# Sums of weight blocks made in DRAM by transfers, five up tiles in seven products

## The chip, the cores and the metric

The kernel runs on one core of a Trainium2 chip. The metric is device time in microseconds, from the launch of the program to its end. A core has TensorE (PE in the profile, its weight loads PEld), VectorE (DVE), ScalarE (ACT), GpSimd (POOL) and SyncE (SP), each with its own queue of instructions, and 16 DMA engines that serve the queues of transfers. Each engine takes its queue in order: an instruction that waits holds up all behind it. In the profile a queue that issues transfers carries a q (SPq, POOLq).

## The reference

One layer of a hybrid block over 512 tokens of width 1024, all in float32: a combined input projection feeds three groups of attention heads (A: differential, B: with forget gates, C: chunked with a relative bias), one output projection, then a gated MLP with a causal depthwise convolution of width 3, then a gated embedding per layer. Cut to what matters here:

```python
def conv_gated_mlp(h, w_up, conv_w, conv_b, w_down):   # w_up 1024 x 5632, w_down 2816 x 1024
    u = h @ w_up
    up = jnp.pad(u, ((0, 0), (CONV_WIDTH - 1, 0), (0, 0)))
    c = conv_b
    for j in range(CONV_WIDTH):
        c = c + conv_w[j] * up[:, j:j + S]
    gate, val = jnp.split(c, 2, axis=-1)
    return (jax.nn.silu(gate) * val) @ w_down

h = x
z = rms_norm(h, ln_mix) @ w_in              # split into the heads of A, B and C
...
h = h + jnp.concatenate([o_a, o_b, o_c], axis=-1) @ w_out
h = h + conv_gated_mlp(rms_norm(h, ln_ffn), w_up, conv_w, conv_b, w_down)
gate = jax.nn.sigmoid(rms_norm(h, ln_ple) @ w_ple_gate)
h = h + (p @ w_ple_proj) * gate
```

## The kernel before

**Numbers.** A float32 product is made of three products in a shorter format. Each operand is split into a rounded part (hi) and a remainder (lo), and `mm3` (line 184) adds hi·hi, hi·lo and lo·hi. For weights ScalarE writes hi (a CAST in the profile) and VectorE the remainder, raw minus hi (a TENSOR_TENSOR w_lo); `split` (line 168) does it for the MLP, `load_w` (line 112) for the attention, where the remainder is at places made by GpSimd or by a transfer that adds.

**Attention.** The input projection is done in ten parts (A0, A0b, A1, A1b, B0 to B2, C0 to C2), each for four tiles of 128 tokens. One part for one token tile is a slot; a slot takes some 6 us. `run` (line 694) puts steps of the attention between the matmuls of a slot; the tables T and EARLY say which step begins in which slot. While one part is multiplied, the weights of the next are loaded by SyncE (`in_w`, four tiles of two blocks each) into a ring of four raw tiles and split. The order of ScalarE, VectorE, GpSimd and SyncE is made by a scheduler here; TensorE's order is that of the program. Normalisation of queries and keys (`qk_sums`, line 367), moves of them (`move`, line 390) and the scaling of probabilities run on GpSimd. Then come the output projection, the norm ahead of the MLP, and the projection of the embedding.

**Up projection.** 22 tiles f, each 128 columns of gate and 128 of value. A plain tile (`up_plain`, line 1237) is two groups of 8 blocks of weights times 3 products over 512 tokens: 48 matmuls of 512 columns. A tile of SEVEN (5, 10 and 15; `up_seven`, line 1261) does the same in the manner of Strassen, seven products of half the rows, half the columns and half the tokens instead of eight: 7 x 4 x 3 = 84 matmuls of 256 columns. It needs sums of weight blocks. `seven_weights` (line 1102) loads five tiles (3584 columns); three transfers on GpSimd's queue add blocks to them while they land (`add_of`), and four additions of GpSimd (`sum_of`) make the rest.

**Down projection.** The 22 tiles are four phases (PHASES 0, 6, 12, 18, 22). For each phase and each half n of the output there are seven products, over as many pairs of tiles as the phase has (18 matmuls of 256 columns, 12 in the last phase), each one added into h by VectorE (`add_h`, line 950). `down_weights` (line 1120) loads four blocks of weights and makes the four differences t1 to t4 on GpSimd (`diff`); each is then split. A difference of the last phase stands in tiles dn_a, dn_b, dn_t. Four products of phase 2 stand behind the last up tile, ahead of the products of phase 3, which need that tile. `cols3` (line 1518) transposes the finished h for the last stage.

**Order in the MLP.** Every piece is a Task. TensorE's order is the order in which tasks are made: `fill`, `downs`, `due` and AHEAD (lines 1470 to 1500) interleave plain pieces with pieces of sevens, and put phases 0 and 1 of the down projection in where their tiles are done. A planner at the end (line 1620 on) lays out the other engines: each task has a due time by TensorE's order, and on each engine the task is taken that can begin soonest, by written costs, and is due first. Raw weights go through a ring of six tiles, split ones through a ring of seven.

Of the kernel before, what the change touches and what calls it, by code (L numbers as in the profile page):

```python
# [8 lines left out]
F32 = mybir.dt.float32  # L9
# [38 lines left out]
AHEAD = 2  # L48

SEVEN = (5, 10, 15)  # L50
# [3 lines left out]
def kernel(ctx: ExitStack, tc: tile.TileContext, x, xt0, xt, pt_in, small, g_ffn_in, bias_c,  # L54
                             w_in, w_out, w_up, w_down, w_ple_gate, w_ple_proj, out):
# [56 lines left out]
    def load_w(src_fn, nk, m, n, name, eng=dve, gain=None, later=False):  # L112
# [3 lines left out]
        for dst, src in src_fn(raw):  # L116
            dma = nc.sync.dma_start(out=dst, in_=src)
            if later:
                tc.keep_in_program_order(dma)
# [247 lines left out]
    def qk_sums(z, t, name):  # L367
# [7 lines left out]
        (dve if name == "A0" else nc.gpsimd).tensor_scalar(rs[:, 0:4], rs[:, 0:4], rstd[:, t, 3:4], EPS, ALU.mult, ALU.add)  # L375
        nc.gpsimd.tensor_tensor(out=rs[:, 4:8], in0=rs[:, 0:4], in1=nhalf[:, 0:4], op=ALU.pow)
# [13 lines left out]
    def move(dst, src):  # L390
        nc.gpsimd.tensor_scalar(dst, f32(src), 1.0, 1.0, ALU.mult, ALU.mult)
# [121 lines left out]
    def head_bias(kind, hd):  # L513

        tb = ap.tile([P, S], F32, tag="bias", bufs=3, name=f"bias_{kind}{hd}")
        if kind == "A":
            nc.gpsimd.tensor_scalar(tb, dist, -SLOPES[hd], 1.0, ALU.mult, ALU.mult)
# [39 lines left out]
    def scores(pr, hh, qbs):  # L557
# [7 lines left out]
        for qb in qbs:  # L565
# [3 lines left out]
            if kind == "A":  # L569
                yield  # L570
                e2, st2 = softmax_map(QK[pr, 1], hh, qb, bq, rowb, f"{pr}_{hh}_{qb}b")
                nc.gpsimd.tensor_scalar(e2, e2, st2[:, 2:3], X["nlam"], ALU.mult, ALU.mult)
                dve.scalar_tensor_tensor(e, e, st[:, 2:3], e2, ALU.mult, ALU.add)
            else:
                nc.gpsimd.tensor_scalar(e, e, st[:, 2:3], 1.0, ALU.mult, ALU.mult)
# [205 lines left out]

    slot = 0
# [14 lines left out]
    for j, (pr, part, *_) in enumerate(PARTS[1:], 1):  # L797
# [18 lines left out]
    for n in range(2):  # L816
        for t in range(NT):
# [9 lines left out]
            slot += 1  # L827
    split_o(7, 8, slice(0, S))
# [101 lines left out]
    L1A, L2A, L2B, L3, L1, L2, L4 = range(7)  # L930
    G, LEFT = {}, {}

    def left_tiles(name):
# [3 lines left out]
    PRODUCTS = ((L1A, 0, "X", True), (L1, 4, "Y", True), (L2, 5, "X", False), (L4, 2, "Y", False),  # L937
                (L3, 6, "X", False), (L2A, 1, "Z", True), (L2B, 3, "X", False))
# [8 lines left out]

    ADDS = {0: ((0, 0),), 1: ((1, 1),), 2: ((0, 1),), 3: ((0, 1),), 4: ((1, 1),), 5: ((0, 0),), 6: ((1, 0),)}

    def add_h(n, j, acc):  # L950
        for b, c in ADDS[j]:
            dve.tensor_tensor(out=hblk(b, n, c), in0=hblk(b, n, c), in1=pv(acc), op=ALU.add)
# [102 lines left out]
    def again(r, name, deps):  # L1055

        w = Weights()
        w.n, w.raw, w.load, w.name = r.n, r.raw, r.load, name
        v = r

        def do():
            w.hi, w.lo = split(v.t, w.n)

        w.hi_slot = Slot("hi")
        w.split = Task("do", [AC(w.n), DV(w.n)], do, (w.load, *deps), [w.hi_slot], [w.raw])
        return w

    def add_of(w, c0, c1, src, deps=(), uses=()):

        def do():  # L1070
            pool.dma_start(out=w.t[:, c0:c1], in_=src(), accum_op=ALU.add)

        return Task("add", [("pool", 0.9), ("acc", (c1 - c0) * 0.0025)], do, (w.load, *deps), (), (w.raw, *uses))

    def sum_of(w, c0, w2, c1, n, deps):

        def do():
            d = w.t[:, c0 : c0 + n]
            pool.tensor_tensor(out=d, in0=d, in1=w2.t[:, c1 : c1 + n], op=ALU.add)

        return Task("do", [("pool", 0.3 + n * 0.0021)], do, (w.load, w2.load, *deps), (), {w.raw: 0, w2.raw: 0})

# [19 lines left out]
    def seven_weights(f):  # L1102

        size = (768, 768, 768, 768, 512)
        ws = [tile_of(n, f"ws{f}_{i}", w_up[f][:, 768 * i : 768 * i + n]) for i, n in enumerate(size)]
        src = w_up[f]
# [4 lines left out]
        for w, deps in zip(ws, ((), (), a, a, b)):  # L1111
            split_of(w, deps)
        order = (0, 1, 4, 3, 5, 6, 2)
# [4 lines left out]
    RIGHT = {"a1": 0, "t1": 4, "t2": 5, "b2": 2, "t3": 6, "a2": 1, "t4": 3}  # L1118

    def down_weights(ph, n, name, tag="raw"):  # L1120

        m = w_down[ph].shape[4]
        src = {what: w_down[ph][n, i, j] for what, (i, j) in (("a1", (0, 0)), ("b1", (0, 1)), ("b2", (1, 1)), ("a2", (1, 0)))}
        raw = {what: tile_of(m, f"{name}_{what}", src.get(what), tag) for what in ("a1", "b1", "b2", "t2", "a2")}

        place = {what: what for what in raw}
        wrote, read = {what: [q.load] for what, q in raw.items()}, {what: [] for what in raw}

        def diff(what, to, a, b):

            a, b, place[what] = place[a], place[b], to

            def do():
                x, y, z = (raw[q].t[:, :m] for q in (to, a, b))
                pool.tensor_tensor(out=x, in0=y, in1=z, op=ALU.subtract)

            q = Task("do", [("pool", 0.3 + m * 0.0021)], do, wrote[a] + wrote[b] + wrote[to] + read[to], (),
                     list({raw[p].raw: 0 for p in (to, a, b)}))
            for p in (a, b):
                read[p].append(q)  # L1140
# [222 lines left out]
    def down(ph, n, tags):  # L1363
        d = Down((ph,), n, tags)
        for what in RIGHT:
            d.product(what)
# [372 lines left out]
```

## Time and profile before

| | us |
|---|---|
| runs, lowest to highest | 727.92 to 728.24 |
| runs, median of 3 | 728.09 |
| profiled execution | 727.97 |
| its span, first to last instruction | 726.2 |
| TensorE busy | 706.1 |
| VectorE busy | 553.0 |
| ScalarE busy | 393.8 |
| GpSimd busy | 270.9 |
| granted TensorE clock | 0.999 |

The span holds the attention up to about 300 us, the MLP from there to about 660, and the gate of the embedding to the end. Line numbers in the profile are those of the kernel; since the engines are called through a helper, most instructions have its line, L78, and are told apart by the names of their tiles: u is the sum of an up tile, s and su those of a tile in seven products, dn_X, dn_Y, dn_Z those of the down projection, w_raw, w_hi and w_lo weights of the MLP, A_r to C_r raw weights of the attention. In a group's row stand, after the bar, the busy time and the mean of one in ns, then the idle time ahead of the group and what ended it.

### The profile page before, as it was taken

The page shows a single profiled execution, that of the slowest core. Times are in us where ns is not written, and L with a number is a line of the kernel's source. Part 1 is how long each engine was busy: PE and PEld are TensorE (multiplying, and loading weights), DVE is VectorE, ACT ScalarE, POOL GpSimd, SP SyncE. Part 2 cuts the span into 40 slices and gives each one's busy share as a digit, 9 for nine tenths or more (in the row PEclk, how much of TensorE's full clock was granted, in tenths as well). Part 3 has the DMA queues.
Part 4 walks back from the last instruction along what each step waited for, and adds up shares of the span by engine and source line. Part 5 has one row for each costly group of instructions (what it writes and reads, how often), then busy time and mean ns, then how long its engine had stood idle before and what let it go on. Part 6 is the DMA issues. An engine that isn't in the chain of part 4 may idle for free. (4 is left out here: it accounts for less than half of the span.)

```text
span 726.2 us, 11876 instructions
## 1 busy us (share of the span) xinstructions
PE 706.1 (97%) x4219; PEld 633.7 (87%) x4219; DVE 553.0 (76%) x1085; ACT 393.8 (54%) x745; POOL 270.9 (37%) x359
## 2 busy tenths in 40 slices
PE   9998999999999999999999999999999999999997
PEld 8987989998999887889888899888998888899886
DVE  7678787887877855758978768787898779988552
ACT  6646775865766664564655544543444543544821
POOL 5676676756665640212101144031520004361400
PEclk9999999999999999999999999999999999999999
DMA  9443425404211135564445434562254322123441
GB/s 332 172 136 110 120 63 124 138 30 110 88 48 56 59 63 165 171 210 90 138 138 125 102 100 123 139 159 66 88 175 117 95 87 82 57 73 94 156 129 58
DMA packets 36806, 83.22 MB, mean 115 GB/s; under 512 B 4198, under 2 KB 5990, under 8 KB 36748
## 3 DMA queue, kind: packets, MB, share of 16 engines
q1 hardware_dynamic: 32700, 73.52, 32.3%
q0 software_dynamic: 3760, 8.66, 6.4%
q8 instruction: 33, 0.54, 0.3%
q10 hardware_dynamic: 288, 0.30, 0.1%
q14 instruction: 25, 0.20, 0.1%
HBM read 74.19 MB, written 4.21 MB: 108 GB/s over the span
## 5 line engine op out<-in xcount | busy, mean ns | idle before, releaser
L78 DVE TENSOR_TENSOR w_lo<-w_raw,w_hi 128x768 fp32r<-128x768 f32 (+1 forms) x118 | 114.9, 993 | 21.9 <-ACT w_hi L78 21.2
L78 ACT CAST w_hi<-w_raw 128x768 fp32r<-128x768 f32 (+1 forms) x118 | 89.6, 786 | 71.1 <-POOL w_raw L78 33.0
L78 PE MATMUL u<-Tl,w_hi 128*128 128x512 f32 (+1 forms) x336 | 125.6, 374 | 0.8 <-DVE Tl L78 0.8
L78 PE MATMUL u<-Th,w_hi 128*128 128x512 f32 (+1 forms) x336 | 125.7, 374 | 0.6 <-ACT pps L78 0.6
L78 PE MATMUL u<-Th,w_lo 128*128 128x512 f32 (+1 forms) x336 | 125.4, 373 | 0.0
L78 POOL TENSOR_TENSOR w_raw<-w_raw,w_raw 128x768 f32<-128x768 f32 (+1 forms) x30 | 55.0, 1854 | 143.7 <-DVE w_lo L78 112.8
L78 PEld LDWEIGHTS u<-Tl,w_hi 128*128 128x128 f32 x336 | 63.1, 188 | 13.0 <-DVE Tl L78 1.2
L78 PEld LDWEIGHTS u<-Th,w_hi 128*128 128x128 f32 x336 | 63.1, 188 | 12.9 <-ACT pps L78 1.0
L78 PEld LDWEIGHTS u<-Th,w_lo 128*128 128x128 f32 x336 | 63.1, 188 | 12.5
L78 DVE SCALAR_TENSOR_TENSOR c<-u,cols,c 128x511 f32<-128x511 f32 x76 | 56.7, 747 | 18.6 <-ACT c L78 17.4
L78 POOL DMA_DIRECT2D w_raw<-in_w_up_dram x9 | 7.9, 912 | 100.2 <-DMA w_raw<-in_w_up_dram 100.2
L78 ACT ACTIVATE c<-u,cols 128x512 f32<-128x512 f32 x38 | 29.5, 776 | 21.7 <-PE u L78 21.7
L78 PE MATMUL dn_X<-w_hi,g_ah 128*128 128x256 f32 x144 | 40.7, 283 | 0.3 <-DVE h L78 0.3
L78 PE MATMUL dn_X<-w_lo,g_ah 128*128 128x256 f32 x144 | 40.7, 283 | 0.3 <-DVE w_lo L78 0.3
L78 PE MATMUL dn_X<-w_hi,g_al 128*128 128x256 f32 x144 | 40.6, 282 | 0.0
L78 PE MATMUL B_z<-B_h,Th 128*128 128x384 f32 x96 | 34.6, 360 | 0.6 <-DVE B_zn L78 0.6
L78 PE MATMUL C_z<-C_h,Th 128*128 128x384 f32 x96 | 34.3, 358 | 0.0
L78 PE MATMUL C_z<-C_l,Th 128*128 128x384 f32 x96 | 32.3, 337 | 0.0
L78 PE MATMUL B_z<-B_h,Tl 128*128 128x384 f32 x96 | 32.3, 337 | 0.0
L78 PE MATMUL C_z<-C_h,Tl 128*128 128x384 f32 x96 | 32.3, 337 | 0.0
L78 PE MATMUL B_z<-B_l,Th 128*128 128x384 f32 x96 | 32.3, 337 | 0.0
L78 PEld LDWEIGHTS dn_X<-w_hi,g_ah 128*128 128x128 f32 x144 | 27.1, 188 | 0.8 <-ACT w_hi L78 0.5
(484 smaller groups left out, 2145.6 us busy)
## 6 DMA issues: line engine op xcount, KB each, us to landing
w_raw<-in_w_up_dram SPq DMA_DIRECT2D x50, 384.0 KB, 3.7
w_raw<-in_w_down_dram SPq DMA_DIRECT2D x24, 384.0 KB, 3.1
w_raw<-in_w_up_dram SPq DMA_DIRECT2D x22, 256.0 KB, 3.4
B_r<-in_w_in_dram SPq DMA_DIRECT2D x12, 384.0 KB, 3.4
C_r<-in_w_in_dram SPq DMA_DIRECT2D x12, 384.0 KB, 3.2
wo_r<-in_w_out_dram SPq DMA_DIRECT2D x16, 256.0 KB, 2.9
w_raw<-in_w_ple_gate_dram SPq DMA_DIRECT2D x16, 256.0 KB, 2.9
h<-in_x_dram SPq DMA_DIRECT2D x4, 512.0 KB, 7.0
```

What stands on the lines that cost most here:

```text
L78: ins = getattr(self.eng, op)(*a, **k)
```

## The change

The sums and differences of weight blocks are added up in DRAM while the attention runs. Nine jobs do it: one for each of five up tiles, one for each of four down phases. A job copies four blocks from DRAM to a DRAM tile on SyncE's queue, then adds four blocks to it by three transfers on GpSimd's queue, one step every three slots. JOBS says in which slots: three jobs begin at slots 10, 11 and 12, three at 18 to 20 and three at 26 to 28. The copies of an up tile move 1.05 MB, those of the phases 3.15 MB each and 2.10 MB for the last one; together 16.8 MB are copied and 16.8 MB added, by nine issues of SyncE and 27 of GpSimd.

In the MLP the weights of a seven are then two loads of weights and three of sums, without transfers that add and without additions; a down product loads its block of weights or of sums (seven loads for each half and phase) and splits it, without subtracts on GpSimd. The form of the seven products of the down projection is another, with as many additions into h, some of them subtracts.

SEVEN is 4, 7, 10, 12 and 15 instead of 5, 10 and 15. TensorE's order in the MLP is written out in a string: P is a piece of a plain tile, S of a seven, D a product of the down projection. Behind the last up tile stand five products of phase 2 instead of four. The transposes cols3 of the first half stand one product further back.

The order of TensorE in the attention stays as it was. In the order that SyncE gets, the copies have no wait of their own: those of the up tiles 4 and 7 and of phase 0 stand between the loads of A1b, those of 10, 12 and 15 between loads of B1, those of phases 1 to 3 among the loads of C0.

```diff
-AHEAD = 2
-SEVEN = (5, 10, 15)
+ORDER = ("PPPPSSPSSSPSPPPPSSPSSSPSPPPDDDDDDDDDDDDDDPSSPSSSPSPSSPSSSPSPPPPSSPSSSPSPDDDDDDDDDDDDDDPPPPPPPPPPPPPPPPP")
+SUMS_FROM, SUMS_STEP = 10, 8
+PLAIN, SEVEN = tiles_of(ORDER)
+JOBS = {}
+_jobs = [("u", f) for f in SEVEN] + [("d", ph) for ph in range(len(PHASES) - 1)]
+_jobs.sort(key=lambda q: q[1] if q[0] == "u" else PHASES[q[1] + 1] + 3)
+for _i, _q in enumerate(_jobs):
+    for _k in range(4):
+        JOBS.setdefault(SUMS_FROM + _i // 3 * SUMS_STEP + _i % 3 + 3 * _k, []).append(_q)
...
+    def sum_job(key):
+        if key[0] == "d":
+            ph = key[1]
+            m = w_down[ph].shape[4]
+            src, more = w_dsum[ph], w_dadd[ph]
+            v = DSUM[ph] = dp.tile([P, 4, 2, m], F32, tag=f"dsum{ph}", name=f"dsum{ph}")
+        else:
+            f = key[1]
+            src, more = w_usum[f], w_up[f][:, 1024:2048].rearrange("p (i c) -> p i c", i=2)
+            USUM[f] = v = dp.tile([P, 4, 512], F32, tag=f"usum{f}", name=f"usum{f}")
+        with tc.issue_after(sp.last):
+            nc.sync.dma_start(out=v, in_=src)
+        for a, what in ((slice(1, 3), lambda: more), (0, lambda: v[:, 1]), (3, lambda: v[:, 0])):
+            yield
+            with tc.issue_after(pool.last):
+                nc.gpsimd.dma_start(out=v[:, a], in_=what(), accum_op=ALU.add, max_dma_last_dim=6144)
+        yield
+
+    def next_job():
+        for key in JOBS.get(slot, ()):
+            if key not in SUMS:
+                SUMS[key] = sum_job(key)
+            next(SUMS[key])
...
             run(in_unit(pr, part, n, t, ws, pre[t]), steps.get(slot, []))
             slot += 1
+            next_job()
...
-    PRODUCTS = ((L1A, 0, "X", True), (L1, 4, "Y", True), (L2, 5, "X", False), (L4, 2, "Y", False),
-                (L3, 6, "X", False), (L2A, 1, "Z", True), (L2B, 3, "X", False))
+    PRODUCTS = {"1e": (0, "X", True, 1, 0, ALU.add), "S1": (3, "Y", True, 0, 1, ALU.subtract), "S2": (4, "X", False, 0, 0, ALU.add),
+                "1o": (2, "Z", True, 1, 0, ALU.add), "1e2e": (5, "X", False, 0, 1, ALU.subtract), "1oS2": (1, "Y", False, 0, 0, ALU.add),
+                "2o": (6, "X", False, 1, 1, ALU.subtract)}
...
     def seven_weights(f):
-        ws = [tile_of(n, f"ws{f}_{i}", w_up[f][:, 768 * i : 768 * i + n]) for i, n in enumerate(size)]
-        a = [add_of(ws[2], 512, 768, lambda: src[:, 1024:1280]), add_of(ws[3], 0, 768, lambda: src[:, 1280:2048])]
-        sums = [(2, 0, 2, 512), (2, 256, 3, 0), (3, 256, 2, 512), (3, 512, 3, 0)]
-        a += [sum_of(ws[i], c0, ws[j], c1, H, a) for i, c0, j, c1 in sums]
-        b = [add_of(ws[4], 0, 512, lambda: src[:, 2048:2560])]
+        usum = USUM[f].rearrange("p i c -> p (i c)")
+        ws = [tile_of(n, f"ws{f}_{i}", w_up[f][:, 768 * i : 768 * i + n] if i < 2 else usum[:, 768 * (i - 2) : 768 * (i - 2) + n]) for i, n in enumerate(size)]
...
     def down_weights(ph, n, name, tag="raw"):
-        def diff(what, to, a, b):
-                pool.tensor_tensor(out=x, in0=y, in1=z, op=ALU.subtract)
...
+        src = {f"{c + 1}{'eo'[i]}": w_down[ph][n, i, c] for i in range(2) for c in range(2)}
+        src.update({what: DSUM[ph][:, i, n] for i, what in enumerate(("S2", "S1", "1e2e", "1oS2"))})
+        return lambda what: split_of(tile_of(m, f"{name}_{what}", src[what], tag))
...
+    FIRST = ("1e", "S1", "1o"), ("1e", "S1")
+    for c in ORDER:
+        next(pieces[c])
...
+    d1.product("1e", (3,))
     cols3(0, 0)
     cols3(1, 0)
-    d1.product("a1", (3,))
+    d1.product("S1", (3,) if "S1" in FIRST[1] else None)
```

More of the change, by code (lines that the diff above doesn't have):

```diff
@@ L827 @@
             slot += 1
+            next_job()
+    assert all(next(q, None) is None for q in SUMS.values())
     split_o(7, 8, slice(0, S))
@@ L945, in pv, with add_h @@
         return t.rearrange("p (b c) -> p b c", b=2)
[L948 to L952, printed above, removed]
+    def add_h(n, what, acc):
+        _, _, _, b, c, op = PRODUCTS[what]
+        dve.tensor_tensor(out=hblk(b, n, c), in0=hblk(b, n, c), in1=pv(acc), op=op)
     ple_cols()
```

184 lines of the change are left out of this document (67 added, 117 removed).

## The prediction

> **What bounds the kernel now.** I read the page's first lines, then busy time by stretches, then the chain of waits, then the groups of each engine, and last the queues and the sequence of SyncE and ScalarE.
>
> ```profile
> span 726.2 us, 11876 instructions
> PE 706.1 (97%) x4219; PEld 633.7 (87%) x4219; DVE 553.0 (76%) x1085; ACT 393.8 (54%) x745; POOL 270.9 (37%) x359
> ```
>
> TensorE is busy for 706.1 of 726.2 us. A change can pay by giving it less work or by closing its 20 us of gaps. Where those lie is in the stretches:
>
> ```profile
> core 0: us, PE busy (x) PEld busy (x) DVE busy (x) ACT busy (x) POOL busy (x), PEclk, DMA share, GB/s
> 40.00:140.00 100.00, 93.36 (x580) 86.46 (x579) 80.28 (x244) 66.21 (x157) 68.19 (x97) 1.00 0.43 112
> 140.00:240.00 100.00, 98.64 (x610) 93.54 (x609) 81.24 (x259) 67.13 (x168) 63.23 (x103) 1.00 0.23 67
> 340.00:520.00 180.00, 180.00 (x1041) 157.34 (x1040) 145.08 (x205) 89.18 (x134) 41.82 (x31) 1.00 0.44 120
> 520.00:540.00 20.00, 19.67 (x166) 19.50 (x165) 18.58 (x22) 8.32 (x12) 8.04 (x4) 1.00 0.47 139
> 540.00:620.00 80.00, 80.00 (x369) 65.48 (x368) 66.22 (x90) 36.43 (x54) 10.17 (x5) 1.00 0.36 107
> 620.00:640.00 20.00, 18.52 (x151) 17.90 (x150) 18.24 (x25) 9.74 (x15) 5.25 (x4) 1.00 0.17 54
> 640.00:660.00 20.00, 19.18 (x164) 18.98 (x163) 17.82 (x19) 9.57 (x15) 14.80 (x8) 1.00 0.12 40
> ```
>
> The clock is 1.00 in each stretch, so a matmul saved is worth its full time. The attention (40 to 240) has 8.0 us of gaps. The up tiles have none: 180.00 of 180.00 and 80.00 of 80.00. The down projection has 0.33 + 1.48 + 0.82 = 2.6 us. What ends those gaps is in the chain of waits (columns: start, length, engine, tile, how many):
>
> ```profile
> 537.44 2.13 PE dn_Y L78 x18
> 539.57 2.14 PE dn_X L78 x18
> 545.99 50.41 PE u L78 x216
> ...
> 628.32 1.12 POOL dn_a L78
> 629.46 0.63 ACT w_hi L78
> 630.12 1.54 DVE w_lo L78
> 631.83 0.35 issue
> 633.68 3.71 PE dn_X L78 x29
> ...
> 651.88 0.69 DVE h L78
> 652.61 0.65 PE n_t L78 x4
> ```
>
> At 628 TensorE waits on a subtract of two weight blocks by GpSimd (dn_a, 1.12 us), then on that block's rounding (w_hi) and remainder (w_lo). At 651.88 it waits for the last addition into h before the transposes n_t. Elsewhere the chain is TensorE itself.
>
> **The change part by part.**
>
> *Two more up tiles in seven products.* 216 matmuls of 512 columns took 50.41 us: 0.2334 each. 18 of 256 columns took 2.14: 0.1189 each. A plain tile has 48 of the first: 11.20 us. A tile in seven products has 84 of the second: 9.98. That is 1.22 less, for two tiles **−2.4 us**, all of it on the path, since TensorE has no gap there. The rest of its work, down projection included, keeps its count.
>
> *What the sevens ask of VectorE.*
>
> ```profile
> L78 DVE TENSOR_TENSOR w_lo<-w_raw,w_hi 128x768 fp32r<-128x768 f32 x85 | 90.8, 1084 | 14.9 <-ACT w_hi L78 14.4
> L78 DVE TENSOR_TENSOR su<-sX,su 128x256 f32<-128x256 f32 x12 | 4.8, 418 | 8.3 <-ACT su L78 8.3
> L78 DVE TENSOR_TENSOR w_lo<-w_raw,w_hi 128x768 fp32r<-128x768 f32 x10 | 9.6, 955 | 3.8 <-ACT w_hi L78 3.7
> L78 POOL TENSOR_TENSOR w_raw<-w_raw,w_raw 128x768 f32<-128x768 f32 x24 | 48.3, 2022 | 139.3 <-DVE w_lo L78 112.8 <-issue 21.7 <-DMA w_raw<-in_w_down_dram 4.4
> L78 POOL DMA_DIRECT2D w_raw<-in_w_up_dram x9 | 7.9, 912 | 100.2 <-DMA w_raw<-in_w_up_dram 100.2
> ```
>
> (The first two rows are of 340 to 660 us, the third of 545 to 598, the POOL rows of the whole run.) Each seven splits 3584 columns of weights instead of 2048: two more remainders of 768, 2 × 0.955 = 1.9, and four additions su of 0.418, 1.7. Together 3.6, for two tiles 7.2 us. VectorE had 180 − 145.08 = 35 us free in 340 to 520. It also gets time back: GpSimd's 24 subtracts (48.3 us) go, and with GpSimd almost still the remainder takes 955 ns, against 1084 in the mean beside them. 85 × 0.13 = 11 us. Net about nothing; I take 0. Without that relief the 7.2 us still fit into the 35 us; they would show only within one seven, at most 9.98 us long, where VectorE has about 12 us to do, and there a plain tile's slack has to follow it.
>
> The Trainium skill, page "GPSIMD Engine Reference", section 1 (Specifications), says that GpSimd shares its SBUF interfaces with VectorE and that instructions of VectorE with two inputs in SBUF contend for them. The 955 and 1084 ns agree; by that rule the relief goes to every such instruction, and the sum stays as it is since TensorE is what ends there.
>
> *Sums ready in DRAM: no subtract ahead of a product.* In the MLP 24 subtracts of GpSimd, three accumulates of each old seven and four additions beside them go, and the same number of columns or more is loaded instead. Down products then need a load and a split, as up tiles do, which show no gap. So the 628 stall loses its first link (1.12 us). Five products of phase 2 rather than four now stand ahead of the first one that needs the last up tile, which covers 2.14 us more. The 651.88 wait gets one product of cover by the move of the transposes behind the next product. Bounds: none of the 2.6 us, or all of it. VectorE is at 18.24 of 20 us in 620 to 640 and becomes what is late next. I take three quarters, **−2.0 us**. More loads in the down projection (seven per half and phase instead of four) lie where the DMA share is 0.44 or below; I take 0.
>
> *GpSimd in the attention.* 27 accumulates are issued from its queue, 0.912 us each by the row above: 25 us more on an engine busy for 68.19 + 63.23 of 200 us. Behind them wait the normalisations and moves of queries and keys that the attention runs on GpSimd. Each accumulate also waits for the step before it to land; with 3 slots between (about 18 us) that wait should be over. Bounds: nothing, or a fifth of it on the path, 5. If the 8.0 us of gaps grow with GpSimd's load, 8.0 × 25 / 131 = **+1.5 us**, which I take.
>
> *Nine copies from DRAM to DRAM on SyncE's queue, 16.8 MB, ahead of weight loads.* No run of before shows such a copy. The nearest rows are the loads at the start, and the accumulates of the output weights (stretches of 10 and 12 us):
>
> ```profile
> q1 hardware_dynamic: 1799, 4.00, 104.5%
> ...
> q0 software_dynamic: 576, 1.05, 54.6%
> ```
>
> The first gives 4.00 MB in 10.45 us of all engines: 383 GB/s. The second 1.05 MB in 6.55: 160 GB/s. So the copies take 44 to 105 us of all engines and the accumulates, as many bytes, 105. The engines are free for 57 + 77 us of 40 to 240 by the shares above, so two of these together do not fit if both are slow, and some work then waits. What can wait are the loads queued behind:
>
> ```profile
> 32.95 3.74 SPq L117 DMA_DIRECT2D A1b_r<-in_w_in_dram  x4
> 39.45 21.80 SPq L117 DMA_DIRECT2D B_r<-in_w_in_dram  x5
> 105.73 10.91 SPq L117 DMA_DIRECT2D C_r<-in_w_in_dram  x4
> ...
> 38.86 0.62 ACT L78 CAST A1b_h<-A1b_r 128x512 fp32r<-128x512 f32 x1 [2.30 <-DMA A1b_r<-in_w_in_dram]
> 39.66 1.15 ACT L78 CAST A1b_h<-A1b_r 128x512 fp32r<-128x512 f32 x2 [0.18 <-issue]
> 57.32 0.83 ACT L78 CAST B_h<-B_r 128x768 fp32r<-128x768 f32 x1
> 139.09 0.39 ACT L78 ACTIVATE B_e<-B_e,B_st 128x128 f32<-128x128 f32 x1
> ```
>
> SyncE issues in order and waits for nothing that a copy needs, so the copies start long before their slots: the first two of the up tiles and the first down phase (1.05, 1.05 and 3.15 MB) stand between the loads of A1b from about 34.6 on, the down phases 1 and 2 (3.15 each) between the loads of C at about 109 and 122. In the same queue the first load of B stands behind 5.8 MB. ScalarE rounds it at 57.32, and softmax work is queued behind ScalarE's wait.
>
> - At 383 GB/s: a load of A1b comes 1.05 MB or 2.7 us later; the second casts are asked for 0.8 us after the first, and the changed order puts them a few short instructions (some 0.9 us) further back: 1.0 late. B's first load lands by 51, on time. Phase 2 is copied by 122 + 8.2 = 130, ahead of ScalarE's need near 139. ScalarE waits 1 us.
> - At 230: A1b 4.6 − 1.7 = 2.9 late, B 34.6 + 25 + 1 = 60.7, 3.4 late, C 0 to 12, middle 6. About 12.3.
> - At 160: 4.9, 14 and some 20. About 39.
>
> Between no part and all of such a wait reaching TensorE (its projections run on weights loaded before), I take half. The copy is nearest to the load: the same queue, the same engines, whole rows. So 1 us, half of it: **+0.5 us**; ends 0 and +19.5.
>
> *Copies, by the skill.* The Trainium skill, page "DMA: Bandwidth & Descriptors", section "Latency and other measured facts", has copies between HBM tensors at 207 to 214 GB/s per direction when nothing slows them. No run of before shows it. By that figure the copies take an estimated 80 us, ScalarE waits about 17 us, and the time would be 727.97 − 2.9 + 8.5 = 733.6 us: the first rival below, which stands on the rows at 160 and 383 without it.
>
> *Sum.* −2.4 − 2.0 + 1.5 + 0.5 = −2.4 us on the profiled execution's 727.97 us (its span 726.2 and 1.8 around it): 725.6. The median of the runs, 728.09, is 0.12 above it, so the same sum stands for both; I say **725.6 us**.
>
> **The rivals.** Runs differ by under 0.2%, some 1.5 us: same is 726.6 to 729.5.
>
> *Late loads (slower).* Copies run nearer 160 than 383 GB/s because they read and write DRAM, and accumulates take their share at the same time. It decides from about 250 GB/s down: B's first load is on time as long as 5.8 MB take under 22 us (266 GB/s). At 230 the sum is 727.97 − 2.9 + 6.1 = 731.2, at 160 744.6. For it: the accumulates, which also move by reading twice, at 160. Against it: ScalarE's present wait of 2.30 us for A1b leaves TensorE's work in 40 to 140 at 93.36, so a wait is not passed on one to one. Chance 0.36.
>
> *Everything in the attention is hidden, the MLP gets all.* −2.4 − 2.6 and the seven tiles' relief let the gaps between sevens stay closed: 721 to 723.3. For it: 8.0 us of gaps with queues half idle. Against it: GpSimd at 68%. Chance 0.12.
>
> *The sevens do not gain.* Three of five sevens stand close together (tiles 10, 12, 15 as 4 and 7 do), VectorE at 12 us against 9.98 in each: five times up to 2 us lost takes the 2.4 and the 2.0. 727 to 729, same. Against it: 35 us free in 180. Chance 0.13; a worse form, where sums land late for the first seven and TensorE stands still, ends at 730 or more, chance 0.05.
>
> **How the numbers follow.** The forecast holds 0.34. Faster: 0.34 + 0.12 = 0.46. Same 0.13. Slower 0.36 + 0.05 = 0.41. Both signs hold much, so the range takes in the upper case but for its far end: 720.5 to 739. The likeliest case alone is 723.5 to 726.6.
>
> **What would show it.** TensorE's matmuls should be 72 more (2 × 84 − 2 × 48) and its busy time after 240 us about 2.4 lower. GpSimd should be nearly without tensor operations after 340, w_lo's mean nearer 955 ns. ScalarE's casts B_h near 57 and C_h near 139 should show no idle time put down to a load; if they show 3 us or more, the late loads have it. The stretch 40 to 240 should hold within 2 us of the old 8.0 us of gaps. I am wrong if copies hold queue q1 above 50 us of all engines, or if the first seven waits for its sums.

## The result and the profile after

The changed kernel takes 758.29 us (median of 4 runs, 755.55 to 760.38) against 728.16 before (median of 4): 1.0404 times as long, 95% interval 1.0387 to 1.0422. The forecast was 725.6 us with a range of 720.5 to 739. The profiled execution took 758.6 us with a span of 756.8.

The page of the kernel after, its first line and its busy times:

```profile
span 756.8 us, 12081 instructions
PE 715.2 (95%) x4291; PEld 641.9 (85%) x4291; DVE 536.2 (71%) x1097; ACT 399.2 (53%) x757; POOL 214.3 (28%) x335
```

TensorE has 72 matmuls more, as forecast, and yet is busy for 9 us longer. Busy time by stretches of the kernel after shows why (columns as in the prediction; the second last is the share of the 16 DMA engines):

```profile
core 0: us, PE busy (x) PEld busy (x) DVE busy (x) ACT busy (x) POOL busy (x), PEclk, DMA share, GB/s
40.00:140.00 100.00, 89.96 (x548) 83.07 (x547) 76.28 (x207) 60.36 (x142) 72.00 (x101) 0.98 0.95 257
140.00:160.00 20.00, 11.55 (x60) 8.77 (x59) 7.79 (x46) 5.07 (x16) 7.44 (x11) 0.93 1.04 281
160.00:180.00 20.00, 14.66 (x75) 12.62 (x74) 11.28 (x39) 11.44 (x28) 9.13 (x15) 0.81 0.86 216
180.00:200.00 20.00, 17.54 (x86) 15.85 (x87) 13.20 (x40) 11.13 (x24) 14.04 (x19) 0.83 0.56 123
200.00:240.00 40.00, 36.04 (x211) 33.52 (x211) 27.88 (x85) 20.35 (x47) 28.93 (x41) 0.96 0.89 189
377.00:557.00 180.00, 180.00 (x1105) 160.25 (x1104) 143.42 (x217) 93.40 (x145) 0.00 (x0) 1.00 0.45 136
650.00:670.00 20.00, 20.00 (x154) 19.21 (x153) 15.09 (x25) 10.40 (x17) 0.00 (x0) 1.00 0.67 218
670.00:690.00 20.00, 20.00 (x172) 20.00 (x171) 15.13 (x22) 8.53 (x13) 0.00 (x0) 1.00 0.36 118
```

The DMA engines are full from 40 to 160 us (0.95 and 1.04; before, 0.43 from 40 to 140 and 0.20 in the next 20). From 140 to 200 TensorE stands still for 16 of 60 us, and the granted clock is 0.81 and 0.83 in the last two of these stretches. Stretches of 4 us show what these means are made of:

```profile
152.00:156.00 4.00, 0.33 (x2) 0.01 (x1) 0.00 (x0) 0.00 (x0) 0.50 (x1) 1.00 1.05 175
156.00:160.00 4.00, 1.83 (x5) 1.06 (x6) 0.00 (x0) 0.06 (x1) 3.83 (x8) 0.67 1.27 395
160.00:164.00 4.00, 1.96 (x8) 1.45 (x8) 1.53 (x3) 3.98 (x9) 2.02 (x3) 0.50 0.74 221
164.00:168.00 4.00, 3.84 (x14) 3.10 (x13) 3.85 (x9) 2.55 (x6) 3.51 (x7) 0.55 0.97 183
176.00:180.00 4.00, 1.26 (x8) 0.94 (x7) 0.07 (x1) 0.24 (x1) 0.00 (x0) 1.00 0.56 173
180.00:184.00 4.00, 2.03 (x6) 1.56 (x7) 2.58 (x15) 0.49 (x2) 3.93 (x6) 0.65 0.11 42
184.00:188.00 4.00, 4.00 (x13) 3.63 (x14) 2.53 (x12) 2.65 (x8) 1.58 (x4) 0.50 0.64 122
```

TensorE stands from about 152 and again from about 177, and each time the clock goes to half some us later, for 10 us in all the first time (0.67, 0.50 and 0.55 of three stretches) and for 7 us the second (0.65 and 0.50). The matmuls that run then are longer. The MLP is as it should be: no gap in the up tiles, none in the down projection any more (650 to 690; before, 0.82 to 1.48 us in each 20), GpSimd at zero.

The chain of waits of the kernel after, at the place of the stall (start, length, what), and ScalarE's waits of the kernel after from 30 to 300 us (total, times, longest):

```profile
117.34 17.31 DMA B_l<-B_r
134.70 25.21 DMA C_r<-in_w_in_dram
159.94 0.83 ACT C_h L103
```

```profile
ACT C_h L103 <- DMA C_r<-in_w_in_dram: 13.6, 2, 9.8
ACT B_e L103 <- DVE B_st L103: 13.5, 10, 6.1
```

A load of C took 25 us and ScalarE stood 9.8 us for it, with softmax work queued behind. Before, this wait does not exist. (B_l<-B_r is one of the attention's own accumulates, on GpSimd's queue; five of them took 17.3 us in the median, 5.7 before.) The DMA queues from 34 to 300 us say what filled the engines (queue, packets, MB, share of 266 us of 16 engines), before:

```profile
q1 hardware_dynamic: 9660, 21.25, 25.9%
q0 software_dynamic: 1728, 4.06, 8.6%
```

and after:

```profile
q0 software_dynamic: 5552, 19.79, 42.0%
q1 hardware_dynamic: 7900, 33.57, 37.8%
```

GpSimd's queue, the accumulates, rose by 33.4% of 266 us, 89 us for 15.7 MB, which is 176 GB/s. (The jobs add 16.8 MB; four older accumulates of 1.05 MB in all lie behind 300 us in the kernel after, which makes the difference.) Where the loss arises and where the gain is can be read off two rows, the first matmuls of the output projection before and after (the last numbers are the first and last start):

```profile
L78 PE MATMUL wo<-wo_h,Th x64: 389/396/483, 241.8 to 306.1; 128*128 128x512 f32 x64
```

```profile
L103 PE MATMUL wo<-wo_h,Th x64: 389/395/483, 279.0 to 343.4; 128*128 128x512 f32 x64
```

The attention lost 37.2 us. From there to the end of the span it was 484.4 us before and is 477.8 now: 6.6 us gained. The two make the 30.6 us by which the spans differ.

### The profile page after: what moved, and what is told of

Its sections match the earlier page's. It is cut to its first block, busy times and chain, and to the rows that moved or that the text cites. A ratio compares the mean times of both kernels' runs of the same rounds, so it can differ in the third digit from the quotient of the medians.

```text
span 756.8 us, 12081 instructions
## 1 busy us (share of the span) xinstructions
PE 715.2 (95%) x4291; PEld 641.9 (85%) x4291; DVE 536.2 (71%) x1097; ACT 399.2 (53%) x757; POOL 214.3 (28%) x335
## 3 DMA queue, kind: packets, MB, share of 16 engines
q0 software_dynamic: 6864, 23.07, 16.7%
## 4 chain that ended last, share of the span: by engine, by line
PE 67%; DMA 11%; DVE 7%; POOL 6%; issue 4%; ACT 3%; SPq 0%; POOLq 0%; DVEq 0%; ACTq 0%
PE u L103 25%; PE dn_X L103 8%; PE pg L103 6%; PE wo L103 4%; PE dn_Y L103 4%; DMA C_r<-in_w_in_dram 3%; PE sX L103 3%; DMA B_l<-B_r 2%; PE dn_Z L103 2%; PE sY L103 2%; PE sZ L103 2%; PE C_z L103 2%; DMA bias_C<-in_bias_c_dram 1%; DMA waq<-in_w_in_dram 1%; PE pp L103 1%
## 5 line engine op out<-in xcount | busy, mean ns | idle before, releaser
L103 DVE TENSOR_TENSOR w_lo<-w_raw,w_hi 128x768 fp32r<-128x768 f32 (+1 forms) x122 | 107.2, 900 | 22.6 <-ACT w_hi L103 22.2
L103 ACT CAST w_hi<-w_raw 128x768 fp32r<-128x768 f32 (+1 forms) x122 | 93.1, 788 | 52.7 <-PE dn_X L103 23.7
L103 PE MATMUL u<-Tl,w_hi 128*128 128x512 f32 (+1 forms) x304 | 112.9, 371 | 0.8 <-DVE Tl L103 0.8
L103 PE MATMUL u<-Th,w_hi 128*128 128x512 f32 (+1 forms) x304 | 112.9, 371 | 0.4 <-ACT pps L103 0.4
L103 PE MATMUL u<-Th,w_lo 128*128 128x512 f32 (+1 forms) x304 | 112.6, 370 | 0.0
L103 DVE SCALAR_TENSOR_TENSOR c<-u,cols,c 128x511 f32<-128x511 f32 x68 | 50.8, 747 | 23.6 <-ACT c L103 22.4
L103 PEld LDWEIGHTS u<-Tl,w_hi 128*128 128x128 f32 x304 | 57.0, 188 | 11.3 <-DVE Tl L103 1.2
L103 PEld LDWEIGHTS u<-Th,w_lo 128*128 128x128 f32 x304 | 57.0, 188 | 11.0
L103 PEld LDWEIGHTS u<-Th,w_hi 128*128 128x128 f32 x304 | 57.0, 188 | 11.0 <-ACT pps L103 0.8
L103 PEld LDWEIGHTS dn_X<-w_lo,g_ah 128*128 128x128 f32 x144 | 27.1, 188 | 0.1
```

What stands on the lines that cost most here:

```text
L103: ins = getattr(self.eng, op)(*a, **k)
```

## The experiments

Two theories at the start. A: loads stand behind copies in SyncE's queue. B: the DMA engines are full, by copies and accumulates together, whatever queue they are in. A third, C, was GpSimd: its 27 issues and their waits.

**No jobs.**

```diff
-    DSUM, USUM, SUMS = {}, {}, {}
+    DSUM, USUM, SUMS = dict(enumerate(w_dsum)), dict(w_usum), {}
-        for key in JOBS.get(slot, ()):
+        for key in ():
```

> Left out: the nine jobs; the weights' sums are read from the inputs without being added up, so the values are not the reference's, while the MLP's instructions and loads are those of the changed kernel. In the changed kernel the first matmul of the output projection starts 37.2 us later than before (279.0 against 241.8), and from there to the end the time is 6.6 us shorter (30.6 us in all). If all of the loss comes from the jobs, the output projection starts near 242 again and the time is 728.2 - 6.6 = 721 to 722 us. If part of the loss comes from the changed order of the engines in the attention, it stays above 724.

Measured: 722.55 us (722.07 to 723.28), ratio 0.9917 (0.9899 to 0.9936); output projection from 243.5. That lies between the two expectations: the start of the output projection is 1.7 us later than before without any job, and the other 35.5 of its 37.2 us come from the jobs. The MLP's gain is real: without the jobs' cost the kernel would be 0.8% faster than before.

**Copies only.**

```diff
-        for a, what in ((slice(1, 3), lambda: more), (0, lambda: v[:, 1]), (3, lambda: v[:, 0])):
-            yield
-            with tc.issue_after(pool.last):
-                nc.gpsimd.dma_start(out=v[:, a], in_=what(), accum_op=ALU.add, max_dma_last_dim=6144)
+        for _ in range(4):
+            yield
```

> Left out: the 27 accumulates; only the nine copies remain, on SyncE's queue among the loads. Theory A, loads stand behind copies in their queue: the load of C that took 25.21 us keeps most of that and the time stays above 740. Theory B, all 16 DMA engines are full by copies and accumulates together (their share is 1.00 to 1.04 from 80 to 160 us): without the accumulates' share there is room, and the time falls to 725 to 732.

Measured: 728.1 us (724.93 to 731.01, 10 runs). Theory A expected over 740 and fails here: the copies alone cost 5.6 us. The profiled execution, one of the shorter with 725.72 us, is 2.4 us longer than that of the run without jobs, and its trace shows where (start, length, what; in brackets the wait ahead of it and what ended it):

```profile
138.68 0.83 ACT L103 CAST C_h<-C_r 128x768 fp32r<-128x768 f32 x1 [1.96 <-DMA C_r<-in_w_in_dram]
141.35 0.36 PE L103 MATMUL B_s<-B_k_k,B_q_q 128*128 128x256 f32 x1 [1.95 <-DVE B_st L103]
```

ScalarE waits 1.96 us for a load of C, the softmax step B_e stands behind it, and TensorE then waits 1.95 us. Queue q1 of this run from 34 to 300 us:

```profile
q1 hardware_dynamic: 10003, 37.94, 43.1%
```

In the run without jobs the same row is

```profile
q1 hardware_dynamic: 9660, 21.25, 25.5%
```

So the copies are 16.7 MB in 17.6% of 266 us, 47 us or 357 GB/s: near the loads' 383.

**Copies on other queues**, all sums made.

```diff
-        with tc.issue_after(sp.last):
-            nc.sync.dma_start(out=v, in_=src)
+        with tc.issue_after(pool.last):
+            nc.gpsimd.dma_start(out=v, in_=src, max_dma_last_dim=6144)
```

> The same bytes, but the nine copies are issued on GpSimd's queue in their slots, so no load stands behind a copy in a queue, and copies and accumulates follow each other. Theory A: most of the 37 us goes, 725 to 735 us. Theory B: the engines still have the same bytes to move in the same stretch, 745 to 760 us. Nine more issues of 0.9 us on GpSimd cost at most 3 us by either.

```diff
-        with tc.issue_after(sp.last):
-            nc.sync.dma_start(out=v, in_=src)
+        with tc.issue_after(act.last):
+            nc.scalar.dma_start(out=v, in_=src)
```

> The same bytes, the nine copies on ScalarE's queue, which is third to SyncE's and GpSimd's. Theory A: 723 to 733 us. Theory B: 745 to 760. Against the run with copies on GpSimd's queue, copies and accumulates can run side by side here, and GpSimd has nothing more to issue.

Measured: 764.16 us on GpSimd's queue (ratio 1.0495, 1.047 to 1.052), 764.73 on ScalarE's (1.0503, 1.0473 to 1.0534). Theory A is gone: no load stands behind a copy, and it is 6 us worse, even above theory B's 745 to 760. The loads are late all the same. Median times to landing with the copies on ScalarE's queue (34 to 300 us; KB each, us):

```profile
B_r<-in_w_in_dram SPq DMA_DIRECT2D x12, 384.0 KB, 13.9
C_r<-in_w_in_dram SPq DMA_DIRECT2D x12, 384.0 KB, 10.7
B_l<-B_r POOLq DMA_DIRECT2D x5, 384.0 KB, 7.5
```

Before, the same loads took 3.4 and 3.2 us. They share the engines, not the queue. Nor is it the order in GpSimd's queue: the accumulates B_l, which stand there among those of the jobs, take 7.5 us here against 17.3 in the changed kernel, and the time is no better.

**Plain transfers for the accumulates.**

```diff
-                nc.gpsimd.dma_start(out=v[:, a], in_=what(), accum_op=ALU.add, max_dma_last_dim=6144)
+                nc.gpsimd.dma_start(out=v[:, a], in_=what(), max_dma_last_dim=6144)
```

> The 27 accumulates become plain transfers of the same bytes on the same queue with the same waits (so the sums are not made and the values are not the reference's). Theory B1, it is the time that an accumulate takes of the engines: in the changed kernel queue q0 took 42.0% of 266 us for 19.8 MB, 8.5% of which were there before, so some 89 us for 15.7 MB (176 GB/s), where the copies alone took 47 us for 16.7 MB (357 GB/s). Plain transfers would take 47 us instead of 94, the stretch of 40 to 240 us is no longer full, and the time falls to 728 to 738. Theory B2, any 16.8 MB more on GpSimd's queue do it, by sharing the engines with the loads: 750 or more.

Measured: 737.74 us (737.09 to 739.02), ratio 1.0126 (1.011 to 1.0141). Same bytes, same queue, same waits, 20.6 us less. GpSimd's queue from 34 to 300 us in this run:

```profile
q0 software_dynamic: 5488, 20.84, 28.4%
```

Without what is there anyway (4.06 MB, 8.5%) that is 16.8 MB in 19.9% of 266 us, 53 us or 317 GB/s, where accumulates went at 176. So it is the engine time of accumulating, theory B1. GpSimd's wait for a step to land is not what differs: its one long wait for a step (usum, up to 300 us) is 9.8 us in the changed kernel and 7.5 here.

**Accumulates of a sixteenth.**

```diff
-                nc.gpsimd.dma_start(out=v[:, a], in_=what(), accum_op=ALU.add, max_dma_last_dim=6144)
+                nc.gpsimd.dma_start(out=v[:, a, ..., :32], in_=what()[..., :32], accum_op=ALU.add, max_dma_last_dim=6144)
```

> The 27 accumulates keep their places, their issues and their order of waits, but move 32 columns of each row, a sixteenth or less of the bytes (the rest of the sums is left out, so the values are not the reference's). Theory B, engine time: the loss goes, as with the copies alone, 725 to 731 us. Theory C, GpSimd: 25 us of issues and its waits for the step before stand in front of the attention's work on GpSimd; then 735 or more remains.

Measured: 733.74 us (733.11 to 736.04), between the two expectations: the great loss goes, 5.6 us above the copies alone stay. Theory C may have a part; the small accumulates are no clean removal of the transfers, since GpSimd's queue still took 14.6% of 266 us, 16 us more than with the copies alone.

**GpSimd alone.** Powers of three columns stand where the accumulates stood.

```diff
-                nc.gpsimd.dma_start(out=v[:, a], in_=what(), accum_op=ALU.add, max_dma_last_dim=6144)
+                pool.tensor_tensor(out=still[:, 3:6], in0=still[:, 0:3], in1=still[:, 0:3], op=ALU.pow)
+    still = cp.tile([P, 6], F32, tag="still", name="still")
+    dve.memset(still, 1.0)
```

> The copies alone, and in the place of each of the 27 accumulates a power of three columns on GpSimd that moves nothing (the sums are not made, so the values are not the reference's); such a power of four columns took 1.1 us in the attention, an issue 0.9. Theory C, GpSimd's time: the output projection starts 6 to 9 us later than with the copies alone (245.9), as it did with accumulates of a sixteenth (254.4), and the time is 732 to 735. Theory D, it was the accumulates' small transfers and the waits for them: within 2 us of the copies alone, 726 to 730.

Measured: 728.88 us (726.91 to 730.18, 10 runs): by the total, theory D. But the rows spoke against it. The output projection of this run:

```profile
L103 PE MATMUL wo<-wo_h,Th x64: 388/389/481, 252.0 to 315.6; 128*128 128x512 f32 x64
```

It starts 6 us later than with the copies alone, and its matmuls have a median of 389 ns where the runs before it have 395 or 396. The edit had also moved something: its new tile takes 24 bytes of each row ahead of the rings of weights, which then lie 32 bytes further on. Repeated without a new tile:

```diff
-                nc.gpsimd.dma_start(out=v[:, a], in_=what(), accum_op=ALU.add, max_dma_last_dim=6144)
+                pool.tensor_tensor(out=nhalf[:, 5:8], in0=nhalf[:, 5:8], in1=nhalf[:, 5:8], op=ALU.pow)
+    dve.memset(nhalf[:, 5:8], 1.0)
```

> As the run with powers in place of the accumulates, but they use free columns of a tile that is there anyway, so the weights lie where they lay (the sums are not made, so the values are not the reference's). Theory C, GpSimd's time costs 6 us: matmuls of 512 columns take 394 ns again and the time is 732 to 735. Theory D, it costs nothing: 727 to 730.

Measured: 734.26 us (733.19 to 736.9). Theory C holds for this part, with the copies there: 27 powers of 0.85 us on GpSimd, 23 us in all, cost 6.2 us over the copies alone. Its row on GpSimd (count; min, median, max in ns; first and last start):

```profile
L103 POOL TENSOR_TENSOR nhalf<-nhalf x27: 837/849/1175, 71.5 to 242.0; 128x3 f32<-128x3 f32 x27
```

The run with the new tile would have given the wrong verdict by its total.

About half of this part goes through the load of C. In this run the load is issued at 129.71 us, 3 us later than with the copies alone, the DMA share is 1.05 from 130 to 140, and ScalarE waits for the load three times as long:

```profile
144.78 0.83 ACT L103 CAST C_h<-C_r 128x768 fp32r<-128x768 f32 x1 [5.96 <-DMA C_r<-in_w_in_dram]
```

That is 4.0 us more, of the 8.4 by which the two profiled executions differ. What GpSimd's time costs without the copies was not tried.

With these the 35.7 us between the run without jobs and the changed kernel divide by medians; the last column is ScalarE's longest wait for a load of C in the profiled execution:

| step | us | more | wait |
|---|---|---|---|
| no jobs | 722.55 | | none |
| copies on SyncE's queue | 728.1 | 5.6 | 1.96 |
| 27 times 0.85 us on GpSimd | 734.26 | 6.2 | 5.96 |
| the accumulates' bytes, plain | 737.74 | 3.5 | 6.66 |
| accumulated | 758.29 | 20.6 | 9.81 |

The runs are of several sessions, in which the kernel before took 727.9 to 728.8, so a step is uncertain by about 1 us. The wait is not the whole of any step: accumulates of a sixteenth took 733.74 with one of 0.69. How far the steps depend on their order was not tried.

**Three sevens.** (No jobs, tiles 4 and 12 of the order plain again.)

```diff
-ORDER = ("PPPPSSPSSSPSPPPPSSPSSSPSPPPDDDDDDDDDDDDDDPSSPSSSPSPSSPSSSPSPPPPSSPSSSPSPDDDDDDDDDDDDDDPPPPPPPPPPPPPPPPP")
+ORDER = ("PPPPPPPPPPPPPSSPSSSPSPPPDDDDDDDDDDDDDDPSSPSSSPSPPPPPPPPPPSSPSSSPSPDDDDDDDDDDDDDDPPPPPPPPPPPPPPPPP")
```

> As the run without jobs (the sums are not made, so the values are not the reference's), but with three tiles in seven products (7, 10 and 15) instead of five; two tiles are plain again. By the pitch of the matmuls that run's 722.5 us get 2.4 us longer: 724.9. If the five sevens gained nothing, because VectorE is late in them, it stays within 0.7 us of 722.5; if they also gained the gaps of the down projection, 726 or more.

Measured: 724.96 us (723.91 to 725.71), 2.4 more than with five.

**Sums spread out.** First into the MLP as fast as they go:

```diff
+    for i, c in enumerate(ORDER):
+        for key, k in LATER.get(i, ()):
+            sum_step(key, k, [q for q in TASKS if q.kind == "pe"][-1])
...
+            with tc.issue_after(behind.ins):
+                if k == 0:
+                    pool.dma_start(out=v, in_=src, max_dma_last_dim=6144)
+                else:
+                    a, what = ((slice(1, 3), more), (0, v[:, 1]), (3, v[:, 0]))[k - 1]
+                    pool.dma_start(out=v[:, a], in_=what, accum_op=ALU.add, max_dma_last_dim=6144)
```

> All sums are made, but only those of up tiles 4 and 7 and of phase 0 in the attention, one step every three or four slots (10 to 42). The other six jobs, copies too, are issued from GpSimd's queue in the MLP, each step behind a named matmul, spread over 336 to 580 us, where the engines' share was 0.36 to 0.44. By theory B the attention keeps 45 us of transfers in 200 instead of 144 and loses 2 to 6 us, and the MLP has 100 us of them in 244 beside its loads: 722 to 729 us, below the kernel before if the attention loses under 5. If in the MLP the loads of weights come late behind the accumulates, 735 or more.

Measured: 741.81 us (735.06 to 742.21), ratio 1.0157 (1.0113 to 1.0202). The order of issue made GpSimd wait for nothing of TensorE's, so the steps followed one another as soon as each landed. Two stretches of this run:

```profile
400.00:460.00 60.00, 55.47 (x378) 51.60 (x377) 40.74 (x59) 25.71 (x38) 6.55 (x8) 0.97 0.97 277
460.00:520.00 60.00, 56.04 (x315) 48.63 (x314) 42.87 (x67) 30.49 (x49) 4.45 (x5) 0.97 0.84 232
```

TensorE has no gap in these stretches without jobs, and loses 4.5 and 4.0 us here. What waited from 395 to 525 us (total, times, longest):

```profile
PE dn_X L104 <- DVE h L104: 4.5, 2, 3.4
PE sX L104 <- DVE su L104: 3.1, 1, 3.1
ACT w_hi L104 <- DMA w_raw<-in_w_down_dram: 11.2, 4, 4.3
```

Almost all of the loss is in the down projection and in a seven, not in the plain up tiles, and ScalarE waits for loads of weights, which it does not do there without jobs. Theory B fits the MLP too.

Then with copies in the attention, later and in pieces, all accumulates in the MLP, and each one held by a real wait: GpSimd first reads one column of the newest split weights.

```diff
+        def do():
+            if w is not None:
+                pool.tensor_scalar(mark, f32(w.lo[:, 0:1]), 1.0, 1.0, ALU.mult, ALU.mult)
+            add_step(key, k)
...
+        for key, i in COPIES.get(slot, ()):
+            v, src, _ = sum_of(key)
+            i = slice(0, 4) if i is None else i
+            with tc.issue_after(sp.last):
+                sp.dma_start(out=v[:, i], in_=src[:, i])
...
-ORDER = ("PPPPSSPSSSPSPPPPSSPSSSPSPPPDDDDDDDDDDDDDDPSSPSSSPSPSSPSSSPSPPPPSSPSSSPSPDDDDDDDDDDDDDDPPPPPPPPPPPPPPPPP")
+ORDER = ("PPPPPPPSSPSSSPSPPPPSSPSSSPSPPPDDDDDDDDDDDDDDPSSPSSSPSPSSPSSSPSPPPPSSPSSSPSPDDDDDDDDDDDDDDPPPPPPPPPPPPPP")
```

(Three plain pieces move from the end to the front. The tables COPIES and ADDS name the slot of each copy and the piece of ORDER behind which each accumulate stands.)

> All sums are made. The copies stay on SyncE's queue in the attention, later and in smaller pieces (slots 20 to 42, one block of a phase at a time). All 27 accumulates move into the MLP, one behind another, each held by a read of the newest split weights, spread over some 320 to 590 us; the sevens are tiles 5, 8, 11, 13 and 16. By the sizes found so far: the 8 us of GpSimd's issues and the 25 us of the accumulates' time leave the attention, which keeps 1 to 5 us of the copies. In the MLP the accumulates need 94 us of the engines in 270 beside a share of 0.44. If that is room enough: 722 to 727 us, faster than before. If accumulates make the loads late wherever they run, the MLP loses 5 to 10 us as in the spread run: 731 to 738.

Measured: 724.97 us (724.41 to 725.25), ratio 0.995 (0.9933 to 0.9967): faster than before by 0.5%.

> As the run before it, with the order of TensorE and the sevens of the changed kernel (4, 7, 10, 12, 15): the six accumulates of tiles 4 and 7 stay in the attention, one every four slots from 26 on, the other 21 go into the MLP. Six issues of 27 cost 1.9 us of the 8.5 found, and 11.8 us of engine time in 130 us some 0 to 2: 1 to 4 us more than with all accumulates in the MLP.

(The same with the changed kernel's ORDER, copies from slot 16 on.)

```diff
+ATTN_ADDS = {26: [(('u', 4), 0)], 30: [(('u', 4), 1)], 34: [(('u', 4), 2)], 38: [(('u', 7), 0)], 42: [(('u', 7), 1)], 46: [(('u', 7), 2)]}
```

Measured: 726.79 us (724.83 to 728.52, 10 runs), 1.8 us more than the run before it. The attention's second hundred microseconds of this run, and of the run before it:

```profile
140.00:240.00 100.00, 94.34 (x576) 88.34 (x575) 77.77 (x242) 62.56 (x152) 62.45 (x99) 1.00 0.47 139
```

```profile
140.00:240.00 100.00, 97.29 (x600) 91.82 (x599) 80.01 (x254) 65.74 (x164) 62.16 (x100) 1.00 0.45 148
```

TensorE has 3 us less there, with the early accumulates and most copies one to four slots earlier; the two were not told apart. All accumulates in the MLP under the same ORDER, most copies up to two slots later than in the run above, and the other accumulates later too (of the table ADDS only the head is shown, and COPIES not):

```diff
-ATTN_ADDS = {26: [(('u', 4), 0)], 30: [(('u', 4), 1)], 34: [(('u', 4), 2)], 38: [(('u', 7), 0)], 42: [(('u', 7), 1)], 46: [(('u', 7), 2)]}
-ADDS = {0: [(('d', 0), 0)], 5: [(('d', 0), 1)], 11: [(('d', 0), 2)],
+ATTN_ADDS = {}
+ADDS = {0: [(('u', 4), 0), (('u', 4), 1), (('u', 4), 2), (('u', 7), 0)], 1: [(('u', 7), 1)], 2: [(('u', 7), 2)], 3: [(('d', 0), 0)],
```

> As the run with all accumulates in the MLP (724.97), but with the changed kernel's own order of TensorE and sevens 4, 7, 10, 12 and 15, and the accumulates of phase 2 and 3 spread to 600 us. Against the run without jobs that one lost 1.9 us behind the start of the output projection, 1.5 of it in 620 to 640. If that came of the moved sevens, 723 to 724.5; if the sums of tile 4 land late, near 340 us, 726 or more.

Measured: 720.37 us (719.55 to 720.77), ratio 0.9887 (0.9868 to 0.9906), below both expectations. Stretches of this run:

```profile
140.00:240.00 100.00, 98.67 (x609) 93.56 (x608) 81.20 (x258) 67.12 (x167) 63.14 (x103) 1.00 0.42 135
400.00:460.00 60.00, 60.00 (x418) 55.66 (x417) 47.94 (x70) 29.46 (x43) 9.67 (x15) 1.00 0.89 215
580.00:660.00 80.00, 80.00 (x527) 72.88 (x526) 62.67 (x94) 39.33 (x60) 0.00 (x0) 1.00 0.41 131
```

All 33.6 MB are moved, and TensorE has the attention of before (98.67 against 98.64) and no gap in these stretches of the MLP. From 300 to 600 us, with the share between 0.74 and 0.89 up to 580, the loads of up weights of 384 KB take 4.9 us to landing, against 3.7 before, and TensorE still has no gap from 340 to 660 us.

**The place of the weights.** One tile of 32 bytes per row ahead of the rings, in this kernel and in the kernel before:

```diff
     gq = cp.tile([P, 8], F32, tag="gq", name="gq")
+    shift = cp.tile([P, 8], F32, tag="shift", name="shift")
+    dve.memset(shift, 0.0)
```

> The kernel with all accumulates in the MLP and the sevens 4, 7, 10, 12 and 15 (720.37), with one more tile of 32 bytes per row ahead of the weight rings, which moves them by 32 bytes. If the place of the weights makes the matmuls of 512 columns 1.3% shorter: 4 to 6 us less, 714.5 to 716.5. If not: 719.5 to 721.

> The kernel before with the same 32 bytes more ahead of its weight rings and nothing else. If the place of the weights does it, it gains the same, 722 to 724.5, and the gain of the best kernel is to be counted against this one. If not: 727.5 to 728.7.

Measured: 716.33 us (715.19 to 717.16), ratio to before 0.984 (0.9826 to 0.9855); and 723.85 us (723.38 to 726.92), ratio 0.995 (0.9935 to 0.9966). The groups of 512 columns in the shifted kernel before (count, busy us, mean ns):

```profile
L78 PE MATMUL u<-Th,w_hi 128*128 128x512 f32 x272 | 106.0, 390 | 0.0
```

and in the kernel before:

```profile
L78 PE MATMUL u<-Th,w_hi 128*128 128x512 f32 x272 | 107.6, 395 | 0.0
```

The rings of weights are the only tiles that the new tile moves. So 716.33 is the best time here, below both kernels; of its 11.6 us against before some 4 belong to the place of the weights, which the kernel before can have as well.

## Why the prediction was wrong

*Two more up tiles in seven products, −2.4.* Right: taking two away cost 2.4 us. VectorE did not get in the way: 143.42 of 180 us busy (before, 145.08), and the remainders of 768 columns in the MLP after are

```profile
L103 DVE TENSOR_TENSOR w_lo<-w_raw,w_hi 128x768 fp32r<-128x768 f32 x90 | 84.2, 953 | 14.9 <-ACT w_hi L103 14.6
```

953 ns, as forecast from 955. The rival of sevens that gain nothing fell with that.

*Sums ready in DRAM, −2.0.* Right in kind, and too small: behind the start of the output projection 6.6 us were gained, 4.2 of them not by the sevens. The 2.6 us of gaps are all closed; where the other 1.6 come from is not settled.

*GpSimd in the attention, +1.5.* Mis-sized. GpSimd's time in the place of the accumulates costs 6.2 us beside the copies, above the step's upper bound of 5. The step scaled the 8.0 us of gaps with GpSimd's load. In the runs a later GpSimd also moved the load of C, and the longer wait for it (5.96 us against 1.96) is part of the cost; the step had no term for that.

*Nine copies on SyncE's queue, +0.5.* The rate was right: near the load, 357 GB/s. The row of the accumulates was the wrong end for it. The price was low: 5.6 us at that rate. The mechanism was right: ScalarE waits for C near 139 with softmax work behind it. But of its 1.96 us TensorE lost 1.95 a moment later, not half.

*The step that failed* is in that part, too: "So the copies take 44 to 105 us of all engines and the accumulates, as many bytes, 105", with what was drawn from it, that the two "do not fit if both are slow". The 105 us were there, from the right row (16.8 MB at the measured 176 GB/s take 95), and so was "some work then waits". But the sum charged the waits to the copies alone and let them hang on the copies' rate. The engine time of the accumulates was put at nothing without a reason: they entered only as 27 issues of GpSimd. Worked out, it was 66 us of transfers that were there in 40 to 240 (43 and 23), 44 of copies and 105 of accumulates by the prediction's own numbers: 215 us for 200, no room at all even with the copies at their best. What the runs showed in its place: accumulating alone, the same bytes on the same queue, costs 20.6 us. The loads of B and C take 8.2 and 5.8 us in the median (3.4 and 3.2 before) and one takes 25, ScalarE stands, TensorE stands, and the granted clock goes to half for 10 and for 7 us. TensorE's busy time is 715.2 us, and without jobs, for the same count, it is

```profile
PE 702.8 (97%) x4291; PEld 635.4 (88%) x4291; DVE 535.0 (74%) x1097; ACT 399.6 (55%) x757; POOL 189.8 (26%) x308
```

So 12.4 us of the loss are matmuls made longer, a term the prediction did not have. By an estimate from the clocks in the first table of stretches (busy time times what the clock is below 1, from 40 to 240 us) some 10 of them are the clock's.

*The signs.* The gaps from 40 to 240 us came to 30.2 us, not within 2 of 8.0, and C_h waits 13.6 us on loads: both signs spoke. The bound on copies, 50 us of all engines, did not: alone they took 47.

*The rivals.* Late loads did win, but not by the mechanism written: not the copies' rate below 250 GB/s, and not the order in the queue, since copies on other queues are no better. It did name the accumulates' share of the engines, but only as something that slows the copies. Its price of 731 to 745 us was short by 14 at the upper end.

*By the skill.* The Trainium skill, page "DMA: Bandwidth & Descriptors", section "Latency and other measured facts", gives 207 to 214 GB/s for copies between HBM tensors at their best; here copies moved 16.7 MB in 47 us of the engines, 357 GB/s. The measurement decides. That page's number is for tiles of other shape. The Trainium skill, page "GPSIMD Engine Reference", section 1 (Specifications), says that VectorE and GpSimd contend for SBUF when VectorE has two inputs there; the 953 ns with GpSimd at rest against 1084 beside it agree.

## What to carry to other kernels

Add up the engine time of every transfer in a stretch, old and new, at the rate of the nearest row of its own kind, and compare the sum with the stretch before looking at queues and order. No one share is the limit: in the MLP TensorE lost time at 0.97 and none at 0.89, and in the attention from 40 to 140 us it lost 4 us at 0.95 and 1 us at 0.78 (copies alone), against the run without jobs. An accumulate took 1.8 times the engine time of a plain transfer of the same bytes on the same queue (176 against 317 GB/s), so put it where the share is low and hold each one with a wait that is real. When a run's total and its rows disagree, look for a second thing the edit moved.

## What was not expected of the hardware

Accumulates from DRAM to DRAM went at 176 GB/s of engine time, plain transfers on the same queue at 317 and copies on SyncE's at 357. The granted clock was at half for 10 us and for 7 us from 156 to 188 us of the kernel after, where TensorE had been busy for 2.2 of the 8 us from 152 and for 3.3 of the 8 us from 176; a mean over 20 us shows 0.81 and 0.83 and hides that. And 32 bytes in the place of the weight tiles change matmuls of 512 columns from 395 to 390 ns and the kernel before by 4 us; in the kernels as built the weight tiles began at a multiple of 32 bytes that is not one of 64, and begin at one of 64 with the shift. Whether that is the rule was not tried with other shifts.
